# One FFN's units issued in written order on every engine, a queue order up to the first gates, and a norm without GpSimd

## The chip, the cores and the metric

The kernel runs as one program on one core of a Trainium2 chip. The core has a matrix engine (TensorE, PE in the rows; its weight loads are listed apart as PEld), three elementwise engines (VectorE = DVE, ScalarE = ACT, GpSimd = POOL), and a sync engine (SP) that here issues the DMAs. Each engine works through its own list of instructions in order; between the lists stand semaphores. The metric is the device time of one execution in microseconds (us), of which three runs of the kernel before gave 3029.19, 3029.55 and 3030.99: a median of 3029.55.

## The reference

One trunk layer of a diffusion backbone over 128 context and 1024 latent positions, 1152 rows of width 1024 in all. What matters here is the first half-step and what follows it:

```
h = modulate(rms_norm(x, norm_ffn1), sh1, sc1)              # sh, sc, g: SiLU(c) @ mod_w + mod_b
x = x + 0.5 * g1 * swiglu(h, ffn1_w_in, ffn1_w_out)          # swiglu: (silu(h @ Wg) * (h @ Wu)) @ w_out
h = modulate(rms_norm(x, norm_mix), sh2, sc2)
proj = h @ w_in                                              # u, v, q, kv, rotary key, two gates of 1024
...
```

The feed-forward width is 2816, so Wg and Wu are 1024 x 2816 each. Everything is fp32; the matrix engine works on a high and a low part of each operand, and a product is the sum of three passes (hi*hi, hi*lo, lo*hi). Each weight is therefore cast once (the high part, ACT, L150) and subtracted once (the low part, L151, POOL by default).

## The kernel before

**Tiling.** The rows lie in three blocks of 384 columns (b = 1, 2, 0 in FFN 1's order), and as two halves of 576. The feed-forward width is cut into 22 tiles of 128, called f. The up projection of a tile f is computed by a Strassen-Winograd scheme: seven products p = 1, 2, 6, 5, 7, 3, 4 of 4 x 128 rows of weights against 576 columns. A product is called a unit here: 24 matmuls of 128x288. For it the kernel forms four sums of the tile's weights on DVE (`make`, L547 to L550), casts the stationary part on ACT (L150) and takes its rest on POOL (L151).

**Stages.** `F1.up` first runs p1 and p2 of the first 9 tiles while the modulation and the first norm are still under way. Then a second loop runs the remaining units: 5 for each of the first 9 tiles, 7 for each of the other 13. Each step of it makes the operands of the unit five ahead, multiplies, drains (`done`) and calls `side1`. Behind it come the down projections (`F1.down`, four groups of tiles: 0 to 6, 7 to 10, 11 to 17, 18 to 21), which multiply the products a (kept in DRAM as `a_d`, loaded again into h10, h11, h20, ... by `a_load` and split by `a_split`) with w_out (`need_w`), and add the result to x (`x_load`). The drain of a down projection is L728. The last group is interleaved with the norm of the mixers (`done1`, `squares`, `norm_h`). Then come the first gate units, three for each block.

**PSUM.** The products of a tile share three pairs of banks in turn. p6 is copied out by ACT (L592) before p7 can use its pair; p7's drain on DVE (L599) must be over before p4 can start; p3 runs between the two on another pair. p1, p5 and p6 are drained by ACT (L592), p2, p7, p3 and p4 by DVE (L595, L599, L603, L613).

**Side work.** From tile 9 on `side1` also steps a generator `mods` that computes the other modulation vectors: 112 loads of 128x512 (`mraw`), for each two multiply-adds (macs) on DVE (L376 for the first, L378 for the others), then a fold over the partitions by two DMAs and two additions on POOL (L914), four transposes on PE (L204) and a sum on DVE (L371). Three steps are taken for each two units. On the last tile, f = 21, `F1.change(p)` runs behind each unit: it loads the first seven a tiles into the buffers of operands that are no longer needed, splits them, loads x, and prepares the first down weights.

**What sets the order.** PE runs in the written order throughout. For the other engines a tile scheduler sorts the instructions by its own estimates of when each is ready; `tc.manual_schedule(engines=...)` takes the named engines out of that, and they then issue in the order in which the program emits. In the kernel before, no other engine is taken out in this stretch.

Of the kernel before, what the change touches and what calls it, by code (L numbers as in the profile page):

```python
# [34 lines left out]
ADD_STEPS = 3  # L35
FOLD_STEPS = {1: 7, 2: 8}
FOLD_AT = 3
POOL_LO = {0: (0, 1, 3, 5), 1: (1, 3, 5, 7), 2: (1, 3, 5, 7)}
QK_SCALE = 192 ** -0.5

HT = T // 2
# [32 lines left out]
def tile_trunk(  # L74
# [314 lines left out]
    class Ffn:  # L389
# [5 lines left out]
        def __init__(self, which, order, wi, wo, early, chunks, wseq):  # L395
            self.which, self.order, self.wi, self.wo, self.early, self.chunks, self.wseq = which, order, wi, wo, early, chunks, wseq
            self.pools, self.hc, self.xq, self.acts, self.xt, self.wts = {}, {}, {}, {}, [], {}
            self.yt = self.ys = None
            self.yring, self.ycount = [], 0
            self.a_d = [dp.tile([P, T], F32, tag=f"a_d{which}_{f}", name=f"a_d{f}") for f in range(FT)]  # L400
            self.ya_d = [dp.tile([P, 2, HT], F32, tag=f"ya_d{which}_{f}", name=f"ya_d{f}") for f in range(early)]

            self.seq = [(f, p) for f0 in range(0, early, 3) for p in (1, 2) for f in range(f0, f0 + 3)]
            self.n_early = len(self.seq)
            self.seq += [(f, p) for f in range(FT) for p in (ORDER if f >= early else ORDER[2:])]
            self.first, self.raws, self.made, self.kept = {}, {}, {}, {}

        def slots(self, pl, *tags):
            for t in tags:
# [159 lines left out]
        def up(self, side):  # L569

            add, mult, early, seq, hc, ys, stores = ALU.add, ALU.mult, self.early, self.seq, self.hc, {}, []
            banks = [ps_two() for _ in range(3)]

            def kept_part(f):

                if f < early:
                    for i in (1, 2):
                        ys[f, i] = self.y_tile()
                        dma(ys[f, i], self.ya_d[f][:, i - 1])

            def silu(y):
                S.activation(out=y, in_=y, func=AF.Silu)

            def done(f, p, ps):
                while stores:
                    dma(*stores.pop())
                if p in (1, 5, 6):
                    y = ys[f, p] = self.y_tile()
                    if f < early:
                        V.tensor_tensor(out=two(y), in0=ps, in1=two(ys[f, 1]), op=add)  # L590
                    else:
                        S.copy(out=two(y), in_=ps)  # L592
                elif p == 2:
                    y = ys[f, 1]
                    V.tensor_tensor(out=two(y), in0=ps, in1=two(y), op=add)  # L595
                    silu(y)
                elif p == 7:
                    y = ys[f, 5]
                    V.tensor_tensor(out=two(y), in0=ps, in1=two(y), op=add)  # L599
                    kept_part(f + 1)  # L600
                elif p == 3:
                    u, y = ys.pop((f, 5)), ys.pop((f, 6))
                    V.tensor_tensor(out=two(y), in0=ps, in1=two(y), op=add)  # L603
                    silu(y)
                    G.tensor_tensor(out=y, in0=y, in1=u, op=mult)
                    stores.append((self.a_d[f][:, HT:T], y))
                else:
                    y = ys.pop((f, 1))
                    if f < early:
                        V.tensor_tensor(out=two(y), in0=ps, in1=two(y), op=add)  # L610
                        G.tensor_tensor(out=y, in0=y, in1=ys.pop((f, 2)), op=mult)
                    else:
                        V.tensor_tensor(out=two(y), in0=ps, in1=two(y), op=mult)  # L613
                    stores.append((self.a_d[f][:, 0:HT], y))
                    if f == FT - 1:
                        dma(*stores.pop())

            for i in range(6):
                self.make(i, V)
            for i0 in range(0, self.n_early, 6):  # L620
                for s in range(2):
                    for i in range(i0, i0 + 6):
                        f, p = seq[i]
                        self.ready(p, s)
                        ps = banks[f % 3]
                        self.product(ps, self.made[i], hc[p], p == 1, (s,))
                        if i % 2 == 0:
                            pair = self.yt.tile([P, 2, MV], F32, tag="ye", name="ye", bufs=3)
                        y = pair[:, i % 2]
                        S.activation(out=y, in_=ps[:, s, :MV], func=AF.Copy if p == 1 else AF.Silu)  # L630
                        dma(self.ya_d[f][:, p - 1, s * MV:s * MV + MV], y)
                        if s == 1:
                            self.make(i + 6)
            for i in range(self.n_early, len(seq)):
                f, p = seq[i]
                self.make(i + 5)
                self.ready(p, 0)
                if i == self.n_early:
                    kept_part(0)
                ba, bb, bc = (banks[(f + n) % 3] for n in range(3))  # L640
                ps = {1: ba, 2: bb, 6: ba, 5: bc, 7: ba, 3: bc, 4: ba}[p]
                self.product(ps, self.made[i], hc[p], p in (1, 2, 5) or (p == 6 and f < early))
                done(f, p, ps[:, :, :MV])
                side(f, p)
# [38 lines left out]
        def change(self, p):  # L683
# [4 lines left out]
            elif p == 2:  # L688
                self.a_load(2, "h20")
                self.a_load(3, "h21")  # L690
                self.a_split(0)
                self.a_split(1)
            elif p == 6:
                self.a_load(4, "h60")
                self.a_load(5, "h61")
                self.a_split(2)
            elif p == 5:
                self.a_load(6, "h50")
                self.a_split(3)
                self.need_w(0, 0)  # L700
            elif p == 7:
                self.x_load(0, "h70")
                self.x_load(1, "h71")
                self.a_split(4)
            elif p == 3:
                self.x_load(2, "h30")
                self.x_load(3, "h31")
                self.a_split(5)
                self.need_w(1, 0)
            else:  # L710
# [237 lines left out]
            F1.change(p)  # L948

    x_block(2)  # L950
    s_ps.close()
    s_ps = ps_pool("ps_w", wide=True)
    clk.later(X_FIRST[0], lambda: x_block(0, gap=gap1))
# [1 line left out]
    clk.flush()  # L955
    s_ps.close()
    s_ps = ps_pool("ps_d", 0, 8)
    into = {1: ("h51", "q0", "q1", "q2"), 2: ("h10", "h11", "h20", "h21", "h60", "h61", "h50"), 3: ("h51", "q0", "q1", "q2")}
    for c in range(3):
        f0, n = F1.chunks[c + 1]  # L960
# [32 lines left out]

    def done1(b, dt):
        if squares(b, dt):
            norm_rest(b, xT[b], r1s[b], 1, mixT, 1.5, 0.48, wait=7)

    win = w_in[0]
    chunk = {}
# [50 lines left out]
    for b in range(NB):  # L1050
        for i in range(3):
# [2 lines left out]
            gate_unit(i, b, loaded[i])  # L1054
            if i == 0:
                F1.x_store(b)
    s_fx.close()
    s_x = ctx.enter_context(ExitStack())
    xp_ = [pool(s_x, "xblocks", side="right")]
# [742 lines left out]
```

## Time and profile before

| | us |
|---|---|
| three runs, median | 3029.55 |
| profiled execution | 3026.47 |
| its span on the chip | 3024.7 |
| units of tiles 9 to 20 (p1 of f = 9 to p1 of f = 21) | 326.74 |
| f = 21 up to the first down projection | 29.36 |
| rest of the down projections up to the mixers' norm | 244.60 |
| the norm's end and the first gates | 73.90 |

The profiled execution is one of its own; its span is what the hardware profiler saw on the core, and 1.8 us lie around it. All positions (as 619.04) are us from the start of the span. A row of a window gives its length, the busy time of each engine with the number of instructions, the granted clock of PE as a share of the full 2.4 GHz, the busy share of the DMA engines and the GB/s moved. A row of the timeline gives the start, the length, the engine, the line and the operation; the bracket is the idle time ahead of it and what released it. A name that ends in a number is one tile.

### The profile page before, as it was taken

What the parts mean: (1) busy time and instruction counts of PE and PEld (TensorE: products, weight loads), DVE (VectorE), ACT (ScalarE), POOL (GpSimd) and SP (SyncE); (2) the same over time, 40 slices, a digit from 0 to 9 for tenths busy, and PEclk for the clock granted to TensorE, in tenths of its full rate; (3) what the DMA queues carried; (4) which work ended last, traced back from release to release, by engine and by line L of the source; (5) the groups of instructions that cost most, each with busy time, mean ns of one, the idle gap of its engine ahead of it and who ended that gap; (6) DMA issues with size and microseconds to landing.
All of it is one profiled execution on the core that took longest, in us unless ns stands there. A gap on an engine that the chain in (4) does not pass through costs nothing.

```text
span 3024.7 us, 47889 instructions
## 1 busy us (share of the span) xinstructions
PE 2880.4 (95%) x19102; PEld 2836.5 (94%) x19102; DVE 1416.5 (47%) x2774; ACT 988.8 (33%) x2073; POOL 990.4 (33%) x663
## 2 busy tenths in 40 slices
PE   7899888999997999999899999999989999999997
PEld 4799888899997999999899999999989999999997
DVE  4644766668526120027537667644364322242313
ACT  5622222232114231104226555521362333341113
POOL 4355445543323011110322212223135544442122
PEclk9999899999998999999999999999989999999999
DMA  8444444475322222211551111255234222244322
GB/s 289 144 128 130 130 125 128 126 246 176 103 72 81 57 64 89 76 35 39 174 152 40 57 32 48 76 181 155 87 124 131 81 66 93 68 157 134 100 71 98
DMA packets 355044, 330.16 MB, mean 109 GB/s; under 512 B 21172, under 2 KB 313380, under 8 KB 354436
## 3 DMA queue, kind: packets, MB, share of 16 engines
q1 hardware_dynamic: 354148, 325.13, 34.5%
q8 instruction: 150, 2.46, 0.3%
q0 software_dynamic: 672, 1.97, 0.2%
q14 instruction: 74, 0.61, 0.1%
HBM read 239.24 MB, written 81.76 MB: 106 GB/s over the span
## 4 chain that ended last, share of the span: by engine, by line
PE 76%; DVE 6%; issue 3%; DMA 2%; ACT 1%; POOL 1%; SPq 0%; DVEq 0%; POOLq 0%; ACTq 0%
PE ps_two L169 25%; PE ps_dn L169 18%; PE ps_up L169 18%; PE ps_w L169 6%; PE ps_s L169 3%; PE ps_s L1380 2%; PE ps_w L204 2%; DVE q L378 2%; DMA mraw<-q 1%; POOL wi L151 1%; PE ps_dn L1127 1%; PE ps_dn L204 1%; DMA mraw<-in_mod_w_dram 0%; DVE t L272 0%; PE ps_b L169 0%
## 5 line engine op out<-in xcount | busy, mean ns | idle before, releaser
L151 POOL TENSOR_TENSOR wi<-raw,wi 128x512 fp32r<-128x512 f32 (+2 forms) x382 | 639.8, 1679 | 1343.7 <-ACT wi L150 1259.7
L169 PE MATMUL ps_two<-h,wi 128*128 128x288 f32 x6336 | 877.2, 299 | 42.5 <-ACT q L592 14.6
L169 PEld LDWEIGHTS ps_two<-h,wi 128*128 128x128 f32 x6336 | 859.4, 191 | 52.8 <-ACT q L592 16.4
L150 ACT CAST wi<-raw 128x512 fp32r<-128x512 f32 (+2 forms) x401 | 290.2, 728 | 1048.9 <-PE ps_two L169 316.6
L169 PE MATMUL ps_dn<-h,wi 128*128 128x384 f32 x2304 | 418.8, 337 | 1.7 <-DVE q L613 1.7
L169 PEld LDWEIGHTS ps_dn<-h,wi 128*128 128x128 f32 x2304 | 402.5, 189 | 2.2 <-DVE q L613 2.2
L169 PE MATMUL ps_up<-h_hi,wi 128*128 128x384 f32 x1152 | 303.4, 340 | 0.0
L728 DVE SCALAR_TENSOR_TENSOR h<-ps_dn,modG,h 128x128 f32<-128x128 f32 (+2 forms) x224 | 108.7, 512 | 278.1 <-PE ps_dn L169 278.0
L169 PEld LDWEIGHTS ps_up<-h_hi,wi 128*128 128x128 f32 x1152 | 211.0, 189 | 0.0
L169 PE MATMUL ps_up<-h_lo,wi 128*128 128x384 f32 x576 | 195.1, 339 | 0.0
L378 DVE SCALAR_TENSOR_TENSOR q<-mraw,s,q 128x512 f32<-128x512 f32 x196 | 189.9, 1020 | 0.1
L169 PE MATMUL ps_two<-q,wi 128*128 128x288 f32 x1056 | 158.4, 309 | 30.0 <-DVE q L599 30.0
L169 PEld LDWEIGHTS ps_two<-q,wi 128*128 128x128 f32 x1056 | 152.8, 202 | 31.5 <-DVE q L599 31.5
L1451 POOL TENSOR_SCALAR p<-p,ast 128x1152 f32<-128x1152 f32 x64 | 79.2, 1237 | 303.6 <-PE ps_w L204 100.1
L169 PE MATMUL ps_up<-wi,h_hi 128*128 128x256 f32 (+1 forms) x864 | 160.8, 286 | 0.0
L169 PE MATMUL ps_dn<-q,wi 128*128 128x384 f32 x720 | 138.1, 338 | 0.0
L169 PE MATMUL ps_s<-kn,qn 128*128 128x384 f32 x576 | 136.9, 346 | 0.0
L150 ACT CAST pt<-ps_w 128x384 fp32r<-128x384 f32 x192 | 86.9, 488 | 145.5 <-PE ps_w L204 145.5
L169 PEld LDWEIGHTS ps_up<-wi,h_hi 128*128 128x128 f32 x864 | 133.6, 188 | 0.0
L169 PEld LDWEIGHTS ps_dn<-q,wi 128*128 128x128 f32 x720 | 126.5, 189 | 0.0
L169 PE MATMUL ps_up<-wi,h_lo 128*128 128x256 f32 (+1 forms) x432 | 122.7, 284 | 0.0
L169 PE MATMUL ps_w<-pt,v 128*128 128x256 f32 x864 | 118.4, 288 | 0.0
(263 smaller groups left out, 4180.3 us busy)
## 6 DMA issues: line engine op xcount, KB each, us to landing
raw<-in_ffn_w_in_dram SPq DMA_DIRECT2D x103, 512.0 KB, 3.9
mraw<-in_mod_w_dram SPq DMA_DIRECT2D x112, 256.0 KB, 2.8
a_d<-q SPq DMA_DIRECT2D x88, 288.0 KB, 2.5
h<-a_d SPq DMA_DIRECT2D x32, 576.0 KB, 8.0
raw<-in_w_in_dram SPq DMA_DIRECT2D x34, 512.0 KB, 3.9
raw<-in_ffn_w_out_dram SPq DMA_DIRECT2D x32, 448.0 KB, 3.8
h<-x_d SPq DMA_DIRECT2D x24, 384.0 KB, 7.6
g_d<-t SPq DMA_DIRECT2D x48, 192.0 KB, 2.1
```

The source lines that it names most:

```text
L150: S.copy(out=hi, in_=src)
L151: (lo_eng or G).tensor_tensor(out=lo, in0=src, in1=f32(hi), op=ALU.subtract)
L169: nc.tensor.matmul(ps, lhsT=l[i], rhs=r[j], start=start and i == j, stop=stop and i == 1, skip_group_check=more)
L204: nc.tensor.transpose(out, in_, ident)
L378: V.scalar_tensor_tensor(out=ac, in0=w, scalar=s2[:, j, cd:cd + 1], in1=ac, op0=ALU.mult, op1=ALU.add)
L728: V.scalar_tensor_tensor(out=xs, in0=ps[:, c0:c1], scalar=modG[:, self.which, cd, dt:dt + 1], in1=xs, op0=ALU.mult, op1=ALU.add)
L1127: nc.tensor.matmul(pm[:, i, :], lhsT=vb[b][:, i, g * P:g * P + P], rhs=wsT[:, g, :], start=True, stop=True)
L1380: nc.tensor.matmul(ps, lhsT=q2[h][:, ts_], rhs=kab[j][:, c0:c1], start=False, stop=j == 1)
L1451: G.tensor_scalar(out=p, in0=p, scalar1=rc, scalar2=0.0, op0=ALU.mult, op1=ALU.add)
```

## The change

The second loop of `up` becomes a function `units`. For FFN 1 it runs under `tc.manual_schedule` for DVE, ACT, POOL and SP, so that they issue in the written order; FFN 2 keeps the scheduler. SP stays in written order from the end of `F1.up` to the end of the first gate units. On the last tile the splits of the a tiles come one or two units later, and the first down weight is asked for after p7 instead of p5. The norm of the mixers computes the low parts of all eight k tiles on DVE (L290), where four of the eight were POOL's (L287) with one more step on ACT. In `done1` the norm's steps of blocks 1 and 2 come later. Code that the diff leaves alone moves five lines down behind the new function, eight behind the new queue order.

```diff
--- before.py
+++ after.py
@@ -35,7 +35,7 @@
 ADD_STEPS = 3
 FOLD_STEPS = {1: 7, 2: 8}
 FOLD_AT = 3
-POOL_LO = {0: (0, 1, 3, 5), 1: (1, 3, 5, 7), 2: (1, 3, 5, 7)}
+POOL_LO = {0: (0, 1, 3, 5), 1: (), 2: (1, 3, 5, 7)}
 QK_SCALE = 192 ** -0.5
 
 HT = T // 2
@@ -404,6 +404,7 @@
             self.n_early = len(self.seq)
             self.seq += [(f, p) for f in range(FT) for p in (ORDER if f >= early else ORDER[2:])]
             self.first, self.raws, self.made, self.kept = {}, {}, {}, {}
+            self.ordered = None
 
         def slots(self, pl, *tags):
             for t in tags:
@@ -631,12 +632,16 @@
                         dma(self.ya_d[f][:, p - 1, s * MV:s * MV + MV], y)
                         if s == 1:
                             self.make(i + 6)
+            self.ready(6, 0)
+            kept_part(0)
+            with tc.manual_schedule(engines=self.ordered) if self.ordered else ExitStack():
+                self.units(seq, banks, done, side)
+
+        def units(self, seq, banks, done, side):
+            hc, early = self.hc, self.early
             for i in range(self.n_early, len(seq)):
                 f, p = seq[i]
                 self.make(i + 5)
-                self.ready(p, 0)
-                if i == self.n_early:
-                    kept_part(0)
                 ba, bb, bc = (banks[(f + n) % 3] for n in range(3))
                 ps = {1: ba, 2: bb, 6: ba, 5: bc, 7: ba, 3: bc, 4: ba}[p]
                 self.product(ps, self.made[i], hc[p], p in (1, 2, 5) or (p == 6 and f < early))
@@ -688,23 +693,23 @@
             elif p == 2:
                 self.a_load(2, "h20")
                 self.a_load(3, "h21")
-                self.a_split(0)
-                self.a_split(1)
             elif p == 6:
                 self.a_load(4, "h60")
                 self.a_load(5, "h61")
-                self.a_split(2)
+                self.a_split(0)
             elif p == 5:
                 self.a_load(6, "h50")
-                self.a_split(3)
-                self.need_w(0, 0)
+                self.a_split(1)
+                self.a_split(2)
             elif p == 7:
                 self.x_load(0, "h70")
                 self.x_load(1, "h71")
-                self.a_split(4)
+                self.need_w(0, 0)
+                self.a_split(3)
             elif p == 3:
                 self.x_load(2, "h30")
                 self.x_load(3, "h31")
+                self.a_split(4)
                 self.a_split(5)
                 self.need_w(1, 0)
             else:
@@ -948,6 +953,7 @@
             F1.change(p)
 
     x_block(2)
+    F1.ordered = {mybir.EngineType.DVE, mybir.EngineType.Activation, mybir.EngineType.Pool, mybir.EngineType.SP}
     s_ps.close()
     s_ps = ps_pool("ps_w", wide=True)
     clk.later(X_FIRST[0], lambda: x_block(0, gap=gap1))
@@ -955,6 +961,8 @@
     clk.flush()
     s_ps.close()
     s_ps = ps_pool("ps_d", 0, 8)
+    s_o = ExitStack()
+    s_o.enter_context(tc.manual_schedule(engines={mybir.EngineType.SP}))
     into = {1: ("h51", "q0", "q1", "q2"), 2: ("h10", "h11", "h20", "h21", "h60", "h61", "h50"), 3: ("h51", "q0", "q1", "q2")}
     for c in range(3):
         f0, n = F1.chunks[c + 1]
@@ -993,7 +1001,7 @@
 
     def done1(b, dt):
         if squares(b, dt):
-            norm_rest(b, xT[b], r1s[b], 1, mixT, 1.5, 0.48, wait=7)
+            norm_rest(b, xT[b], r1s[b], 1, mixT, (1.5, 6.0, 8.0)[b], 0.48, wait=7)
 
     win = w_in[0]
     chunk = {}
@@ -1054,6 +1062,7 @@
             gate_unit(i, b, loaded[i])
             if i == 0:
                 F1.x_store(b)
+    s_o.close()
     s_fx.close()
     s_x = ctx.enter_context(ExitStack())
     xp_ = [pool(s_x, "xblocks", side="right")]
```

Three places of the order. The first is DVE in the units of one tile f, from the start of the sums or the drain of p2 (L595 before, L596 after) on; L547 to L550 (L548 to L551 after) are the sums of the next tile, L599 (L600) is p7's drain, which p4 waits for. Before:

```order
L547 TENSOR_TENSOR s_3228<-raw 128x512
L378 SCALAR_TENSOR_TENSOR q_1202<-mraw,s_114,q_1202 128x512
L595 TENSOR_TENSOR q_1201<-ps_two,q_1201 128x576
L548 TENSOR_TENSOR raw<-raw 128x512
L378 SCALAR_TENSOR_TENSOR q_1202<-mraw,s_114,q_1202 128x512
L549 TENSOR_TENSOR raw<-s_3228,raw 128x512
L378 SCALAR_TENSOR_TENSOR q_1202<-mraw,s_114,q_1202 128x512 x4
L550 TENSOR_TENSOR raw<-raw 128x512
L378 SCALAR_TENSOR_TENSOR q_1202<-mraw,s_114,q_1202 128x512 x5
L599 TENSOR_TENSOR q_1201<-ps_two,q_1201 128x576
L603 TENSOR_TENSOR q_1201<-ps_two,q_1201 128x576
L613 TENSOR_TENSOR q_1201<-ps_two,q_1201 128x576
```

After:

```order
L596 TENSOR_TENSOR q_1201<-ps_two,q_1201 128x576
L378 SCALAR_TENSOR_TENSOR q_1202<-mraw,s_114,q_1202 128x512 x4
L548 TENSOR_TENSOR s_3230<-raw 128x512
L549 TENSOR_TENSOR raw<-raw 128x512
L550 TENSOR_TENSOR raw<-s_3230,raw 128x512
L551 TENSOR_TENSOR raw<-raw 128x512
L600 TENSOR_TENSOR q_1201<-ps_two,q_1201 128x576
L378 SCALAR_TENSOR_TENSOR q_1202<-mraw,s_114,q_1202 128x512
L376 TENSOR_SCALAR q_1202<-mraw,s_114 128x512
L604 TENSOR_TENSOR q_1201<-ps_two,q_1201 128x576
L376 TENSOR_SCALAR q_1202<-mraw,s_114 128x512
L614 TENSOR_TENSOR q_1201<-ps_two,q_1201 128x576
```

Between the drain of p2 and that of p7 stood ten macs and three of the sums; now there are four macs and the four sums, or in about every second tile five macs, the four sums and a short group from L371 on. The other macs stand behind the drains of p7, p3 and p4.

The second is SP at the end of the units. `raw<-in_ffn_w_out` is a weight of the down projection, h10 and on are buffers that receive the a tiles, h70 and h71 receive x. Before:

```order
L88 DMA a_d19_134<-q2_1201 128x576
L88 DMA raw_5827<-in_ffn1_w_out_dram 128x7x128
L88 DMA mraw_2907<-q3_1202 64x512 x2
L88 DMA mraw_2903<-in_mod_w_dram 128x512
L88 DMA a_d20_135<-q2_1201 128x576
L88 DMA mraw_2904<-in_mod_w_dram 128x512
L88 DMA a_d20_135<-q2_1201 128x576
L88 DMA raw_5911<-in_ffn1_w_out_dram 128x7x128
L88 DMA h10_5716<-a_d0_115 128x1152
L88 DMA h11_5718<-a_d1_116 128x1152
```

After:

```order
L88 DMA mraw_2909<-q3_1202 64x512 x2
L88 DMA mraw_2908<-in_mod_w_dram 128x512
L88 DMA h50_5821<-a_d6_121 128x1152
L88 DMA h70_5853<-x_d0_71 128x2x384
L88 DMA h70_5853<-x_d1_72 128x2x384
L88 DMA h70_5853<-x_d2_73 128x2x384
L88 DMA h71_5857<-x_d0_71 128x2x384
L88 DMA h71_5857<-x_d1_72 128x2x384
L88 DMA h71_5857<-x_d2_73 128x2x384
L88 DMA raw_5861<-in_ffn1_w_out_dram 128x7x128
L88 DMA mraw_2905<-in_mod_w_dram 128x512
```

The first weight of the down projection stood ahead of all loads of a tiles; now it stands behind seven of them and the six loads of x into h70 and h71, which have to wait until PE is done with p7.

The third is DVE in the norm of the mixers, ahead of the sum L230 of block 1's squares, for which PE's transposes wait; L290 (h_lo0) are the low parts of block 0, L728 (L733) are drains of the last down projections. Before:

```order
L272 SCALAR_TENSOR_TENSOR t384_8258<-h31_5905,modA_112,t384_8176 128x128
L272 SCALAR_TENSOR_TENSOR t384_8258<-h31_5905,modA_112,t384_8176 128x256
L290 SCALAR_TENSOR_TENSOR h_lo0_8182<-t384_8247,modT_111,h_hi0_8181 128x128
L290 SCALAR_TENSOR_TENSOR h_lo0_8182<-t384_8247,modT_111,h_hi0_8181 128x256
L728 SCALAR_TENSOR_TENSOR h31_5905<-ps_dn_8243,modG_113,h31_5905 128x384
L728 SCALAR_TENSOR_TENSOR h71_5863<-ps_dn_8280,modG_113,h71_5863 128x384
L226 TENSOR_TENSOR r1_8140<-r1_8140,t384_8277 128x384
L230 TENSOR_TENSOR r1_8138<-r1_8138,r1_8140 128x384
```

After:

```order
L290 SCALAR_TENSOR_TENSOR h_lo0_8187<-t384_8252,modT_111,h_hi0_8186 128x128
L290 SCALAR_TENSOR_TENSOR h_lo0_8187<-t384_8252,modT_111,h_hi0_8186 128x256
L290 SCALAR_TENSOR_TENSOR h_lo0_8187<-t384_8262,modT_111,h_hi0_8186 128x128
L290 SCALAR_TENSOR_TENSOR h_lo0_8187<-t384_8262,modT_111,h_hi0_8186 128x256
L733 SCALAR_TENSOR_TENSOR h31_5905<-ps_dn_8248,modG_113,h31_5905 128x384
L733 SCALAR_TENSOR_TENSOR h71_5857<-ps_dn_8285,modG_113,h71_5857 128x384
L733 SCALAR_TENSOR_TENSOR h30_5901<-ps_dn_8315,modG_113,h30_5901 128x384
L226 TENSOR_TENSOR r1_8145<-r1_8145,t384_8282 128x384
L733 SCALAR_TENSOR_TENSOR h30_5901<-ps_dn_8332,modG_113,h30_5901 128x384
L230 TENSOR_TENSOR r1_8143<-r1_8143,r1_8145 128x384
```

Ahead of L230 stood eight low parts of block 0, and now there are sixteen, and two drains more.

## Rows read from the trace of the kernel before

**Rows 1.** Windows: stretch, length, busy time by engine, PE clock, DMA share, GB/s.

```profile
292.30:619.04 326.74, 287.85 (x2047) 285.33 (x2046) 227.28 (x272) 85.62 (x143) 163.78 (x113) 0.93 0.42 125
619.04:648.40 29.36, 24.23 (x171) 23.77 (x169) 26.24 (x24) 14.91 (x18) 12.05 (x7) 0.94 0.80 276
648.40:893.00 244.60, 244.60 (x1420) 244.35 (x1421) 139.72 (x220) 40.31 (x47) 75.87 (x44) 1.00 0.47 145
893.00:966.90 73.90, 55.42 (x305) 54.29 (x304) 53.29 (x112) 35.34 (x71) 28.05 (x22) 0.88 0.27 86
885.00:907.00 22.00, 22.00 (x129) 22.00 (x128) 8.79 (x20) 5.18 (x9) 4.34 (x4) 1.00 0.44 138
```

**Rows 2.** Timeline, DVE, units at the full clock: drains of p7 of two tiles.

```profile
205.38 0.76 DVE L599 TENSOR_TENSOR q<-ps_two,q 128x576 f32<-128x576 f32 x1 [2.42 <-PE ps_two L169]
...
221.48 0.76 DVE L599 TENSOR_TENSOR q<-ps_two,q 128x576 f32<-128x576 f32 x1 [2.42 <-PE ps_two L169]
```

**Rows 3.** Waits, 292.3 to 647.5: total us, times, longest.

```profile
PE ps_two L169 <- DVE q L599: 28.5, 5, 6.2
...
DVE s L547 <- DMA raw<-in_ffn_w_in_dram: 28.1, 7, 6.0
...
PE ps_two L169 <- ACT q L592: 14.6, 5, 4.3
```

**Rows 4.** Timeline, 310 to 328: DVE and PE around one drain of p7.

```profile
312.40 0.74 DVE L378 SCALAR_TENSOR_TENSOR q<-mraw,s,q 128x512 f32<-128x512 f32 x1
...
313.86 6.86 DVE L378 SCALAR_TENSOR_TENSOR q<-mraw,s,q 128x512 f32<-128x512 f32 x4
...
321.44 5.55 PE L169 MATMUL ps_two<-q,wi 128*128 128x288 f32 x24 [6.04 <-DVE q L599]
```

**Rows 5.** Lines by form, 292.3 to 647.5: busy us, mean ns, idle before, releaser.

```profile
L378 DVE SCALAR_TENSOR_TENSOR q<-mraw,s,q 128x512 f32<-128x512 f32 x136 | 137.9, 1067 | 0.1
...
L548 DVE TENSOR_TENSOR raw<-raw 128x512 f32<-128x512 f32 x12 | 10.1, 839 | 0.6
...
L371 DVE TENSOR_REDUCE msum<-ps_dn 128x8 f32<-128x512 f32 x7 | 4.8, 686 | 6.1 <-PE ps_dn L204 6.1
...
L151 DVE TENSOR_TENSOR h<-h 128x1152 fp32r<-128x1152 f32 x7 | 10.5, 1536 | 2.7 <-ACT h L150 2.6
...
L150 ACT CAST h<-h 128x1152 fp32r<-128x1152 f32 x7 | 7.7, 1149 | 0.0
...
L204 PE MATMUL ps_dn<-ident,mraw 128*128 128x128 f32 x28 | 4.2, 272 | 0.0
```

**Rows 6.** Timeline, 616 to 650: the last tile and the first down projection.

```profile
619.04 12.85 PE L169 MATMUL ps_two<-h,wi 128*128 128x288 f32 x96
...
625.63 0.95 ACT L150 CAST wi<-raw 128x896 fp32r<-128x896 f32 x1 [2.06 <-issue]
...
641.19 8.50 SPq L88 DMA_DIRECT2D h<-x_d  x12
...
648.35 1.83 PE L169 MATMUL ps_dn<-h,wi 128*128 128x384 f32 x9 [0.85 <-DVE q L613]
```

**Rows 7.** DMA issues, 600 to 680: KB each, median us to landing.

```profile
raw<-in_ffn_w_out_dram SPq DMA_DIRECT2D x8, 448.0 KB, 6.2
```

**Rows 8.** Timeline, 918 to 958: the mixers' norm and PE's waits.

```profile
921.74 2.53 POOL L151 TENSOR_TENSOR wi<-raw,wi 128x1024 fp32r<-128x1024 f32 x1
...
922.51 3.04 DVE L290 SCALAR_TENSOR_TENSOR h_lo<-t,modT,h_hi 128x128 fp32r<-128x128 f32 x2
...
927.53 0.73 DVE L290 SCALAR_TENSOR_TENSOR h_lo<-t,modT,h_hi 128x128 fp32r<-128x128 f32 x2
...
930.93 0.90 PE L204 MATMUL ps_dn<-ident,r 128*128 128x128 f32 x3 [9.28 <-DVE r L230]
...
946.66 0.38 PE L242 MATMUL ps_dn<-ones,r 128*128 128x1 f32 x2 [4.19 <-POOL r L226]
...
951.68 2.29 PE L242 MATMUL ps_dn<-ones,r 128*128 128x1 f32 x10 [4.63 <-DVE r L226]
```

## The prediction

> **What bounds the kernel now.** I read the windows first, stage by stage. In the down projections PE is busy for 244.60 of 244.60 us at the full clock: nothing can be won there [rows 1]. In the two stages ahead of it and in the one behind it PE has gaps, and those are the stages that the change touches.
>
> The units of tiles 9 to 20 take 326.74 us, with PE busy for 287.85 and a granted clock of 0.93 [rows 1]. What they need is seen where no engine was late: two drains of p7 lie 221.48 - 205.38 = 16.10 us apart with five units between them, so a unit is 3.22 us at the full clock [rows 2]. From p1 of f = 9 to p1 of f = 21 there are 12 x 7 = 84 units, 270.5 us, and 28 transposes of 4.2 us in all [rows 5], of which I count 3.6: 274.1. So 52.6 us are lost: 38.9 idle, and 13.7 in matmuls at the lower clock, which is granted after idle time.
>
> The waits say who is late: p4 waits for p7's drain (28.5 us, longest 6.2), and p7 for the copy of p6 (14.6) [rows 3]. The timeline shows why. DVE does macs from 313.86 for 6.86 us without a gap, then the drain, and PE starts p4 6.04 us late and then takes 5.55 us for 24 matmuls instead of 3.22 [rows 4]. DVE isn't short of time: it is busy for 227.28 of 326.74 us [rows 1]. It has the wrong work in front.
>
> The last tile takes 29.36 us up to the first down projection [rows 1], for 7 x 3.22 = 22.5 us of work: 6.9 lost. In the norm and the first gates, PE is busy for 55.42 of 73.90 us [rows 1]: 18.5 idle. Its 305 instructions there take 0.182 us on average; just before they take 22.00 / 129 = 0.171 [rows 1]; the difference, 3.4 us, is the lower clock. Lost: 21.9. Nearly all the idle time is three waits: 9.28 us for L230 of block 1, 4.19 and 4.63 for L226 of block 2 [rows 8].
>
> **The change part by part.**
>
> *The units in written order.* Between p2's drain and p7's there were ten macs and three sums, 10 x 1.07 + 3 x 0.84 = 13.2 us [rows 5], with idle time for data on top; now four macs and four sums, 7.6 us, or with a fifth mac and a group from L371 (0.69 [rows 5], and four short operations that I put at 1.6) 11.0. PE needs 3 x 3.22 = 9.66 us from p2's end to p7's, and p3 covers one more unit before p4 needs the drain: 12.9 us, less the drains of p2 and p7, each 0.76 [rows 2], leaves 11.4. The light tiles have 3.8 us to spare and the heavy ones 0.4, so I expect some waits of about 1 us in the heavy ones: 4 us in the stretch with what they cost in clock. In total DVE would be busy for 227.28 and POOL for 163.78 us of about 278 [rows 1], 82% and 59%. Gain: 52.6 - 4 = 48.6. The bounds: everything lost comes back (52.6), or nothing does (0); 48.6 is near the first because the work between two drains now fits, by rows.
>
> Here a rule speaks against the change. The pair L290 takes 0.73 us where POOL is quiet and 3.04 where POOL does a 2.53 us subtraction beside it [rows 8]; likewise a mac takes 0.74 us in one place and 1.07 on average [rows 4, 5]. The Trainium skill ("SBUF — State Buffer", section "SBUF: two separate sides") has it that GpSimd and a VectorE operation with two SBUF inputs exclude each other on a shared port pair for the whole instruction. If POOL's same work lies in 278 us instead of 327, the waiting part of the macs, 136 x 0.33 = 45 us [rows 4, 5], would grow by 327/278 to 53: some 8 us more on DVE, of which only the heavy tiles' share, about 4, would reach PE. By this estimate the gain would be 45.
>
> *The end of the units.* Before, the first down weight was cast at 625.63, 6.6 us after p1 of f = 21 began [rows 6]. Now its load stands on SP behind the six loads of x into h70 and h71, which wait for p7: 5 x 3.22 = 16.1 us after p1. Twelve such issues took 8.50 us [rows 6], so six take 4.3: the weight is issued at 20.4 and lands after 6.2 [rows 7] at 26.6. Then everything is in order. On ACT: its cast 0.95 [rows 6], then that of h21, 1.15 [rows 5]: 28.7. On DVE: the split of h21, 1.54 [rows 5], and p3's drain: 31.0. ACT's silu (put at a drain's length) and the casts of h60 and h61 end at 34.0, DVE's three macs in between at 34.2, its two splits at 37.3, and only then p4's drain, 38.0, on whose bank the first down projection waits. If the load takes as long as it did where the queue was emptier, everything is some 2 us earlier; I take 37. PE has nothing to do from 22.5 on, so it idles 14.5 us, and after such a gap the clock is low for a while: the 9.28 us gap cost 1.9 of the 3.4 us above, so 2. New: 39, against 29.4: a loss of 10. The bounds: a gain of 6 (no wait at all) and a loss of 12.
>
> *The queue order on SP in the down projections* moves loads only where PE waits for none [rows 1]; the cover is one weight's load of 6.2 us [rows 7] beside 30 us for eight steps of it. Nothing; if the cover is gone, one load.
>
> *The norm.* PE ran dry at 930.93 - 9.28 = 921.65 [rows 8]. Block 1's step comes 4.5 later on the kernel's own clock of PE work (6.0 instead of 1.5), so PE arrives at 926.2. DVE has four pairs of L290 more ahead of L230, 2.9 us at 0.73, and is spared part of the 2.3 us that POOL cost a pair [rows 8]: L230 ends between 931 and 934. The wait is 5 to 8, say 6. Block 2's step comes 6.5 later, and both its waits, 8.8 us [rows 8], are over by then. Left: 6, about 2 for transposes and products that wait for each other, 2 for the clock: 10 of 21.9, a gain of 12 (6 to 19).
>
> The sum: 48.6 - 10 + 12 = 50.6. The profiled execution took 3026.5; 2975.9 on its base. The median of three runs is 3.1 above it: 2979.
>
> **The rivals.**
>
> *A, DVE stays behind.* The written order puts each weight's sums and splits where they must wait for loads and POOL in turn, and an in-order engine can't use such a wait. If each of 12 tiles still loses 3 us, 36 us of the gain are gone: 3015. For it: DVE waits for weights 28.1 us in the units already [rows 3], and the heavy tiles have 0.4 us to spare. Against it: the light ones have 3.8.
>
> *B, the boundary costs nothing*, because x or the weight lands sooner or the next bank is free: 10 back, and 3 to 5 from the old gap: 2965. For it: the load itself is short. Against it: p4's drain stands behind the splits whatever the load does.
>
> *C, slower.* One mechanism: the four sums stand ahead of p7's drain, and the first of them reads a weight whose load stands on SP behind the store of an a tile, which waits for POOL's product. A late weight then holds p7's drain, and so PE, in each tile. A wait for a weight was up to 6.0 us [rows 3]. At 6.0 for each of 12 tiles, PE would lose 72 us and, as in the stall above, about 2.3 in clock each time, 28: 100 instead of 52.6, so with the other two terms 3029.6 + 47 + 10 - 12 = 3075. It decides from 4.4 us a tile on, clock included, thus from a wait of about 2.1: there (4.4 x 12 = 52.6) the units gain nothing, and the other two terms nearly cancel. For it: the queue is now strictly in order. Against it: the load of the weight is asked for a whole tile ahead.
>
> *D, no change.* If the scheduler's order was near the written one where it matters, and the stalls come from the amount of work, the units stay at 326.7 and the time at 3029.6 + 10 - 12 = 3028. Against it: ten macs between two drains became four or five.
>
> **How the numbers follow.** The forecast (2979) has 0.55, A 0.18, B 0.14, C 0.08, D 0.05. The forecast's own range goes from 2968 (gates at their best) to 2992. The range of 8 in 10 takes in B and A and leaves out C, D and the edges: 2958 to 3018. Runs of this kernel differ by 1.8 us, and 0.2% or 6 us is about what can be told from no change. Faster by more: the forecast, B and nearly all of A, 0.87. Same: D and a part of C, 0.05. Slower: 0.08.
>
> **What would show it.** The units from p1 of f = 9 to p1 of f = 21: 278 us with a clock above 0.98, and waits of PE for p7's drain under 10 us. If that window is above 300, A; above 327, C. A gap of PE of 12 to 16 us ahead of the first down projection, ended by p4's drain; none, B. The window from the norm's begin to the end of the first gates of the last block 12 us shorter, with one wait for L230 of 5 to 8 us. What would make it wrong: waits of PE for weights' casts or splits, which before had none of length, or a second stage that is slower although nothing in it was moved.

## The result

The changed kernel takes 2983.09 us (median of four runs, 2980.64 to 2986.1) against 3029.37 of before (3025.32 to 3030.99): a ratio of 0.985, 95% interval 0.9833 to 0.9867. It is faster by 46 us; 50 were forecast (2979), and the time lies inside the range.

The two traces divide the kernel at the same instructions: p1 of f = 9, p1 of f = 21, the first down projection, the first sum of squares of the mixers' norm (L242) and the first matmul of 128x256 behind the gates. Windows of the changed kernel (length, busy time of PE, PEld, DVE, ACT, POOL, clock, DMA share, GB/s), first the units, then the last tile, the down projections, and the norm with the gates:

```profile
290.89:567.06 276.17, 272.76 (x2047) 272.29 (x2045) 212.71 (x250) 84.77 (x142) 160.30 (x111) 0.99 0.44 138
567.06:610.41 43.35, 22.37 (x171) 22.17 (x169) 26.60 (x25) 15.71 (x19) 16.22 (x9) 0.80 0.88 294
610.41:862.00 251.59, 251.59 (x1451) 251.34 (x1452) 161.91 (x246) 41.67 (x49) 78.62 (x44) 0.99 0.45 135
870.78:944.06 73.28, 64.08 (x364) 62.92 (x364) 52.33 (x118) 33.54 (x65) 15.20 (x9) 0.95 0.32 108
```

The last of these as it was before:

```profile
907.16:991.61 84.45, 65.97 (x365) 64.84 (x365) 51.17 (x102) 38.39 (x77) 27.74 (x21) 0.90 0.26 84
```

| stretch | before | after | gain | forecast |
|---|---|---|---|---|
| up to p1 of f = 9 | 292.29 | 290.89 | 1.4 | 0 |
| units of tiles 9 to 20 [rows 1, first] | 326.75 | 276.17 | 50.6 | 48.6 |
| last tile [rows 1, second] | 29.31 | 43.35 | -14.0 | -10 |
| down projections up to L242 | 258.81 | 260.37 | -1.6 | in the -10 |
| norm and gates | 84.45 | 73.28 | 11.2 | 12 |
| the rest of the span | 2033.1 | 2034.8 | -1.8 | 0 |
| sum | | | 45.8 | 50.6 |

In the units PE is idle for 276.17 - 272.76 = 3.4 us, where it was 38.9, and the granted clock is 0.99 instead of 0.93. All that PE waits for between the units and the gates in the changed kernel (total us, times, longest):

```profile
PE ps_dn L169 <- DVE q L614: 21.0, 1, 21.0
PE ps_dn L169 <- DVE h L733: 6.6, 1, 6.6
PE ps_two L169 <- ACT q L593: 3.3, 1, 3.3
PE ps_dn L204 <- DVE st L213: 2.2, 1, 2.2
PE ps_dn L242 <- DVE r L226: 0.4, 1, 0.4
```

No wait for p7's drain is left ([rows 3] had 28.5 us). Of the waits for a copy, 14.6 us in [rows 3], one of 3.3 is left. They were named after ACT, but in four of the five (12.5 us) it was p6's copy, and that stood on ACT behind the silu (L582) of p2's result, which waited for p2's drain on DVE, and that stood behind macs. The longest of the four, before the change:

```profile
625.15 6.95 DVE L378 SCALAR_TENSOR_TENSOR q<-mraw,s,q 128x512 f32<-128x512 f32 x7
...
632.02 0.74 DVE L595 TENSOR_TENSOR q<-ps_two,q 128x576 f32<-128x576 f32 x1
...
632.80 0.68 ACT L582 ACTIVATE q<-q 128x576 f32<-128x576 f32 x1 [6.22 <-DVE q L595]
633.39 2.19 ACT L150 CAST h<-h 128x1152 fp32r<-128x1152 f32 x2
...
635.48 0.63 ACT L592 COPY q<-ps_two 128x576 f32<-128x576 f32 x1
...
636.16 8.17 PE L169 MATMUL ps_two<-h,wi 128*128 128x288 f32 x48 [4.28 <-ACT q L592]
```

The macs did get longer, as the argument on the shared port had it: by form, between 290.89 and 605 us,

```profile
L378 DVE SCALAR_TENSOR_TENSOR q<-mraw,s,q 128x512 f32<-128x512 f32 x117 | 134.1, 1186 | 6.6 <-DMA mraw<-in_mod_w_dram 6.6
L548 DVE TENSOR_TENSOR s<-raw 128x512 f32<-128x512 f32 x12 | 12.6, 1049 | 0.0
L376 DVE TENSOR_SCALAR q<-mraw,s 128x512 f32<-128x512 f32 x18 | 11.2, 644 | 0.0
```

so 145.3 us for 135 macs (L378 and L376), 1.08 each, where the 136 and 20 of before took 137.9 ([rows 5]) and 21.2, 1.02 each. The rise is that of L378, which reads two tensors: 1186 ns instead of 1067. L376, which reads one, fell from 1072 to 644. No L378 of this stretch without a POOL instruction beside it took more than 0.75 us. That agrees with the Trainium skill ("SBUF — State Buffer", section "SBUF: two separate sides"): with POOL's work in less time, more macs meet it. It cost DVE some 14 us in L378 (117 x 0.119), where 8 were estimated, and some 8 over all macs (135 x 0.06). PE's waits show none of it, where 4 were put down to it.

The one loss is the last tile. The timeline, from the loads of x on to the first down projection:

```profile
583.12 4.19 SPq L88 DMA_DIRECT2D h<-x_d  x6
587.35 0.47 SPq L88 DMA_DIRECT2D raw<-in_ffn_w_out_dram  x1
...
596.76 0.94 ACT L150 CAST wi<-raw 128x896 fp32r<-128x896 f32 x1 [14.02 <-DMA raw<-in_ffn_w_out_dram]
597.60 1.15 ACT L150 CAST h<-h 128x1152 fp32r<-128x1152 f32 x1
...
598.78 2.34 DVE L151 TENSOR_TENSOR h<-h 128x1152 fp32r<-128x1152 f32 x1 [13.11 <-ACT h L150]
601.04 0.74 DVE L604 TENSOR_TENSOR q<-ps_two,q 128x576 f32<-128x576 f32 x1
601.71 3.21 DVE L378 SCALAR_TENSOR_TENSOR q<-mraw,s,q 128x512 f32<-128x512 f32 x3
...
604.85 4.75 DVE L151 TENSOR_TENSOR h<-h 128x1152 fp32r<-128x1152 f32 x2
...
609.52 0.74 DVE L614 TENSOR_TENSOR q<-ps_two,q 128x576 f32<-128x576 f32 x1
...
610.41 5.82 PE L169 MATMUL ps_dn<-h,wi 128*128 128x384 f32 x23 [20.98 <-DVE q L614]
```

The first down weight is issued behind six loads of x, 20.3 us after p1 of f = 21, and lands 9.4 us later. ACT has waited 14.02 us for it, with the cast of h21 behind it; DVE has waited 13.11 us for that cast, with p3's drain, three macs, two splits and p4's drain behind it; and PE has waited 20.98 us for p4's drain. It is the chain that was forecast, link by link, but it ends 43.35 us after p1 instead of 38.0 (37 was taken): 3.2 for the load (9.4 instead of 6.2), and about 2 for splits that take 2.3 us each instead of 1.54.

In the norm, the wait that remained is not the one that was named:

```profile
890.26 4.14 DVE L290 SCALAR_TENSOR_TENSOR h_lo<-t,modT,h_hi 128x128 fp32r<-128x128 f32 x6
894.32 1.65 DVE L733 SCALAR_TENSOR_TENSOR h<-ps_dn,modG,h 128x384 f32<-128x384 f32 x3
894.98 1.33 PE L169 MATMUL ps_dn<-h,wi 128*128 128x384 f32 x3 [6.59 <-DVE h L733]
...
905.57 0.54 PE L204 MATMUL ps_dn<-ident,st 128*128 128x128 f32 x3 [2.24 <-DVE st L213]
```

Six low parts (L290) stand in a row in front of three drains (L733), and PE waits 6.59 us for the first of these, since the bank that it is to write next must be drained by it. L230 follows while PE works. The waits for block 2 ([rows 8]: 4.19 and 4.63) are gone.

### The profile page after: what moved, and what is told of

It is laid out like the page before. It is cut to its first block, busy times and chain, and to the rows that moved or that the text cites. A ratio compares the mean times of both kernels' runs of the same rounds, so it can differ in the third digit from the quotient of the medians.

```text
span 2978.9 us, 47869 instructions
## 1 busy us (share of the span) xinstructions
PE 2862.8 (96%) x19102; PEld 2821.9 (95%) x19102; DVE 1429.3 (48%) x2790; ACT 982.6 (33%) x2061; POOL 980.5 (33%) x651
## 4 chain that ended last, share of the span: by engine, by line
PE 81%; DVE 3%; issue 2%; DMA 1%; POOL 1%; ACT 1%; SPq 0%; DVEq 0%; POOLq 0%; ACTq 0%
PE ps_two L169 29%; PE ps_dn L169 18%; PE ps_up L169 18%; PE ps_w L169 6%; PE ps_s L169 3%; PE ps_s L1389 2%; PE ps_w L204 2%; POOL wi L151 1%; DMA h<-a_d 1%; PE ps_dn L1136 1%; PE ps_dn L204 0%; PE ps_b L169 0%; ACT q L461 0%; DVE h_lo L290 0%; DMA raw<-in_ffn_w_in_dram 0%
## 5 line engine op out<-in xcount | busy, mean ns | idle before, releaser
L169 PEld LDWEIGHTS ps_dn<-h,wi 128*128 128x128 f32 x2304 | 403.7, 189 | 29.2 <-ACT wi L150 21.2
L733 DVE SCALAR_TENSOR_TENSOR h<-ps_dn,modG,h 128x128 f32<-128x128 f32 (+2 forms) x224 | 108.8, 512 | 268.9 <-PE ps_dn L169 268.8
L378 DVE SCALAR_TENSOR_TENSOR q<-mraw,s,q 128x512 f32<-128x512 f32 x196 | 206.1, 1094 | 9.6 <-DMA mraw<-in_mod_w_dram 9.5
L169 PE MATMUL ps_two<-q,wi 128*128 128x288 f32 x1056 | 146.9, 294 | 1.6 <-DVE q L600 1.6
L169 PEld LDWEIGHTS ps_two<-q,wi 128*128 128x128 f32 x1056 | 142.1, 188 | 1.8 <-DVE q L600 1.8
```

Source lines behind the costliest of these rows:

```text
L169: nc.tensor.matmul(ps, lhsT=l[i], rhs=r[j], start=start and i == j, stop=stop and i == 1, skip_group_check=more)
L378: V.scalar_tensor_tensor(out=ac, in0=w, scalar=s2[:, j, cd:cd + 1], in1=ac, op0=ALU.mult, op1=ALU.add)
L733: V.scalar_tensor_tensor(out=xs, in0=ps[:, c0:c1], scalar=modG[:, self.which, cd, dt:dt + 1], in1=xs, op0=ALU.mult, op1=ALU.add)
```

## The experiments

All were timed beside the kernel before on the same chip. Twelve kernels, each from the changed kernel unless said otherwise.

### Which part brings what

**The units alone.** The norm, its steps and SP's order behind the units as before.

```diff
-POOL_LO = {0: (0, 1, 3, 5), 1: (), 2: (1, 3, 5, 7)}
+POOL_LO = {0: (0, 1, 3, 5), 1: (1, 3, 5, 7), 2: (1, 3, 5, 7)}
...
-    s_o = ExitStack()
-    s_o.enter_context(tc.manual_schedule(engines={mybir.EngineType.SP}))
...
-            norm_rest(b, xT[b], r1s[b], 1, mixT, (1.5, 6.0, 8.0)[b], 0.48, wait=7)
+            norm_rest(b, xT[b], r1s[b], 1, mixT, 1.5, 0.48, wait=7)
...
-    s_o.close()
```

> The changed kernel with the mixers' norm, its steps and the queue order after the units as before; only the units (with their new placing on the last tile) are in written order. Theory: the two parts add up. The units give back 50 us, the end of the last tile costs 14 to 16, and the gates stay at their old 22 us of loss: time 2993 to 2996. Rival: the gates gain from the earlier arrival of something in the units or in the queue order too; then the time is under 2990.

2992.76 us, ratio 0.9877 (0.9859 to 0.9895). The units take 276.1 us, the last tile 44.4, norm and gates 84.5, as before. The time is just under the theory's 2993 to 2996, and the parts are as it had them.

**The gates alone.** `change` and the scheduling of the units as before.

```diff
-    F1.ordered = {mybir.EngineType.DVE, mybir.EngineType.Activation, mybir.EngineType.Pool, mybir.EngineType.SP}
...
```

> The reverse: units and last tile as before (scheduled), and only the mixers' norm on DVE, its later steps and the queue order after the units. Theory: 11 us better than before, all of it between the first sum of squares and the third gate unit: 3018 to 3020, with the units at 326 us. Rival: the gates' part of the gain hangs on the units' order; then within 4 us of before.

3014.34 us, ratio 0.9951 (0.9936 to 0.9967). Norm and gates take 73.5 us, the 11 expected; another 4 come from the last tile (25.2 us instead of 29.3), where the scheduler placed things otherwise, which was not expected and puts the time 4 us under the theory's 3018 to 3020. The units take 325.0 us, and the stalls of before are there:

```profile
PE ps_two L169 <- DVE q L600: 29.3, 6, 6.4
PE ps_two L169 <- ACT q L593: 11.3, 5, 3.0
```

**The steps and the low parts, one by one.** First the low parts on POOL again, then the steps at 1.5 again.

```diff
-POOL_LO = {0: (0, 1, 3, 5), 1: (), 2: (1, 3, 5, 7)}
+POOL_LO = {0: (0, 1, 3, 5), 1: (1, 3, 5, 7), 2: (1, 3, 5, 7)}
```

> The changed kernel with the mixers' norm as before (four of eight low parts on POOL), the later steps kept. Theory: most of the gates' 11 us comes from the later steps (block 2's two waits are gone by them alone), and the low parts on DVE bring at most 3 us, since the sixteen of block 0 now hold the drain L733 that PE waits 6.6 us for: time 2980 to 2986. Rival: POOL's subtraction beside DVE's two-operand operations is what made the norm late; then 2988 or more.

```diff
-            norm_rest(b, xT[b], r1s[b], 1, mixT, (1.5, 6.0, 8.0)[b], 0.48, wait=7)
+            norm_rest(b, xT[b], r1s[b], 1, mixT, 1.5, 0.48, wait=7)
```

> The changed kernel with the norm's steps at 1.5 for all blocks again, the low parts on DVE kept. Theory: block 2's two waits (4.2 and 4.6 us before) and block 1's 9 us come back for the most part, since PE reaches them early again: 2990 to 2994. Rival: the low parts on DVE alone make the sums ready in time; then 2983 to 2986.

With the low parts on POOL: 2988.07 us (2980.37 to 2989.48), and 73.2 us for norm and gates, the same as the changed kernel's 73.3. The wait for the drain is shorter, but a wait for L230 is added:

```profile
PE ps_dn L169 <- DVE h L733: 4.1, 1, 4.1
PE ps_dn L204 <- DVE r L230: 2.6, 1, 2.6
```

In the trace the stretch that this edit touches is as long as without it. But the traced execution is the fastest of the four (2980.37); the others took 2987.19 to 2989.48, so the median lies 5 us above the changed kernel's, and where those 5 us are no trace shows. With the steps at 1.5: 2996.33 us (2991.33 to 3001.14), 2 us over the theory's range, and 84.2 us for norm and gates, with waits like those of before back:

```profile
PE ps_dn L204 <- DVE r L230: 9.3, 1, 9.3
PE ps_dn L242 <- DVE r L226: 5.6, 2, 5.3
PE ps_dn L242 <- POOL r L226: 3.0, 1, 3.0
```

So, by the traces, the later steps are the whole gain of this part (84.2 to 73.3), and neither the low parts on DVE nor SP's order, which the last kernel keeps, adds to it. Whether the low parts are worth anything to the whole time stays open: the traced execution falls where the theory had it (2980 to 2986), and the median where the rival had it (2988 or more).

### Whose order matters in the units

```diff
-    F1.ordered = {mybir.EngineType.DVE, mybir.EngineType.Activation, mybir.EngineType.Pool, mybir.EngineType.SP}
+    F1.ordered = {mybir.EngineType.DVE}
```

> The changed kernel with only DVE in written order in the units; ACT, POOL and SP are scheduled. Theory: DVE's order (four or five macs instead of ten between the drains of p2 and p7) is what took the stalls away, so the units stay near 276 to 285 us, and only the last tile changes with the order of the loads: 2970 to 2992. Rival: the loads' or the casts' order is as necessary; then PE waits again for drains or weights and the units take over 300 us, time above 3005.

In the other, `{DVE, Activation, Pool}`:

> The changed kernel with DVE, ACT and POOL in written order in the units and SP scheduled. Theory: the same units (276 to 280 us), since PE never waited for a load there; the last tile's gap stays if the scheduler too puts the first down weight behind the loads of x, and shrinks if not: 2968 to 2985. Rival: the scheduler sends the loads of the macs in bunches of eight, so that DVE, now bound to the written order, waits for weights or macs and p7's drain is late: units over 290 us.

DVE alone: 2964.99 us, ratio 0.9785 (0.977 to 0.9801). Without SP: 2966.46 us, 0.9791 (0.9773 to 0.9808). Both are faster than the changed kernel. PE's busy time between 290 and 560 us in both, DVE alone first:

```profile
290.00:560.00 270.00, 268.57 (x2034) 268.10 (x2034) 214.62 (x243) 88.08 (x143) 165.89 (x111) 1.00 0.47 139
```

```profile
290.00:560.00 270.00, 269.93 (x2047) 269.70 (x2046) 213.72 (x251) 85.69 (x144) 159.99 (x111) 1.00 0.47 140
```

From p1 of f = 9 to p1 of f = 21 they take 271.6 and 269.9 us. Both came out better than expected, in time (2970 to 2992 and 2968 to 2985) and in the units (276 us at least). DVE's order is enough to take the stalls away: the wait for p7's drain is gone in both, and 1.3 and 0 us are left of the waits for a copy. Whether the order of the other three without DVE's would do the same was not run, nor were the macs moved by themselves. The written order of ACT and POOL costs nothing in the units, and that of SP costs 6 us: in the changed kernel the store of an a tile stands on SP behind a weight's load, goes out at 295.29 us, and ACT's copy of p1 in the first tile has to wait for its landing. So PE waits 3.34 us before p6, and then has a granted clock of 0.83 between 300 and 320 us. Of the 17 to 18 us over the changed kernel, most lie in the last tile: 28.5 and 30.4 us instead of 43.4, since SP, scheduled, loads the first down weight early again.

### What holds PE in the last tile

Two theories: the weight's load holds ACT's queue and all behind it, or the splits of h60 and h61 in front of p4's drain hold DVE. The weight at p5 as before, then in front of all loads at p1, then only the splits moved, then the weight at p1 and the splits moved:

```diff
             elif p == 5:
                 self.a_load(6, "h50")
+                self.need_w(0, 0)
...
             elif p == 7:
...
-                self.need_w(0, 0)
```

> The changed kernel with only the first down weight asked for after p5 again (it was after p7). Theory: the 21 us gap ahead of the first down projection comes from that weight's load, which stood behind six loads of x and held ACT's queue, and with it DVE's. Now it is issued at about 13 us after p1 of the last tile, lands some 6 to 9 later, and holds the casts of h11 and h20 in the meantime, so p4 starts up to 6 us late, but the rest follows at once: first down projection at 33 to 36 us instead of 43.3, time 2974 to 2977. Rival: the splits of h60 and h61 ahead of p4's drain hold PE whatever the weight does; then the gap shrinks by less than 4 us and the time stays at 2980 to 2983.

```diff
             if p == 1:
+                self.need_w(0, 0)
                 self.a_load(0, "h10")
...
             elif p == 7:
...
-                self.need_w(0, 0)
```

> The changed kernel with only the first down weight moved to the front of what p1 of the last tile issues (ahead of all loads of a tiles). Theory: with the weight there early nothing holds ACT; p4's drain still stands behind three macs and the splits of h60 and h61 on DVE, so PE waits some 5 us instead of 21: first down projection at about 27 us after p1, time about 2966. Rival (the splits in front of the drain are the cause, not the weight): the wait stays above 15 us and the time at 2980 or more.

```diff
             elif p == 3:
...
-                self.a_split(4)
-                self.a_split(5)
                 self.need_w(1, 0)
             else:
+                self.a_split(4)
+                self.a_split(5)
                 self.a_split(6)
```

> The changed kernel with only the splits of h60 and h61 moved behind p4's drain; the weight stays behind the loads of x. Theory (the weight): p3's drain still stands behind the split of h21, whose cast waits on ACT behind the weight's; p4's drain comes some 5 us earlier than in the changed kernel, but PE then waits for the splits instead: 2979 to 2983. Rival (the splits): the gap falls to under 6 us, time about 2968.

The fourth kernel has the second and the third of these edits.

> Both edits: the weight in front at p1, the splits of h60 and h61 behind p4's drain. Theory: the first down projection starts within 3 us of p4's end (25 us after p1), but the splits of h60 and h61 now stand behind a sum (L371) that waits for PE's transposes, so PE waits 2 to 5 us for h60 within the first down projection. Time 2962 to 2967, the same as with the weight alone or up to 4 us better.

Times and lengths in us; the last tile is counted from p1 of f = 21 to the first down projection.

| | time | last tile | PE's waits there |
|---|---|---|---|
| changed kernel | 2983.09 | 43.4 | 21.0 |
| weight at p5 | 2980.0 | 41.5 | 11.2 + 5.1 |
| weight at p1 | 2968.44 | 30.0 | 7.6 |
| splits moved | 2977.98 | 39.4 | 17.0 |
| both | 2973.99 | 25.4 | 3.0, and 6.3 + 1.7 later |

The weight at p1 decides it: 13 of the 21 us go, as the theory of the weight said (2966 expected, 2968 measured; the first down projection at 30.0 us, where about 27 were expected). The splits alone are worth 4 us of the wait, where it had 5; the wait for the splits that it expected in their place did not come, and the time is 1 us under its range. The weight at p5 came 3 us above its range, at a time that the rival had named. The trace shows another cause than the rival's: p4 was to start up to 6 us late and it was 11, since the load took 9.3 us there and ACT held the casts of h11 and h20 behind it. PE's two waits in that kernel:

```profile
PE ps_two L169 <- DVE q L600: 11.2, 1, 11.2
PE ps_dn L169 <- DVE q L614: 5.1, 1, 5.1
```

The same mechanism spoils the kernel with both edits. Its first down projection starts early, after a wait of 2.95 us, but the casts of h60 and h61 now stand on ACT behind that of the *second* down weight, which is late in the same way:

```profile
604.97 0.94 ACT L150 CAST wi<-raw 128x896 fp32r<-128x896 f32 x1 [15.71 <-DMA raw<-in_ffn_w_out_dram]
605.81 3.25 ACT L150 CAST h<-h 128x1152 fp32r<-128x1152 f32 x3
...
607.01 0.69 PE L169 MATMUL ps_dn<-h,wi 128*128 128x384 f32 x1 [6.35 <-ACT h L150]
```

It was expected at 2962 to 2967 and came in at 2973.99; the wait for h60 was expected behind a sum on DVE (L371), and it came from ACT. In these kernels ACT was held by whichever weight's cast had a late load.

### Further than the changed kernel

With DVE alone in order, p4's drain stands behind macs and splits. Without macs behind p7 and p3 of the last tile:

```diff
-        if f >= F1.early:
+        if f >= F1.early and not (f == FT - 1 and p in (7, 3)):
             some(*MOD_UP)
```

> DVE alone in written order in the units, and no macs of the modulation behind p7 and p3 of the last tile (they run in the down projections instead). Theory: p4's drain stood behind three macs and two splits on DVE, 3.2 and 3.1 us, and PE waited 5.9 us for it; without the macs it waits 2 to 3 and nothing else is late: 2961 to 2963, against 2965 with DVE alone in written order. Rival: the drain waits for the loads and casts of h60 and h61, not for DVE's time; then 2964 to 2966.

2963.29 us (2959.95 to 2966.28), ratio 0.9783 (0.9768 to 0.9797). The last tile takes 27.6 us; the wait for p4's drain is 4.0 us, where 2 to 3 were expected, and waits of 0.7 us are added. It has the lowest median of all, but is not clear of the kernel with DVE alone (2964.99; ratios 0.9783 and 0.9785), so time doesn't tell the theory (2961 to 2963) from its rival (2964 to 2966). The trace has the drain behind p3's drain and two splits on DVE, 4.25 us, without a wait for a load, as the theory had it.

Then the steps of block 0's norm spread out, to bring the drains forward:

```diff
-            norm_rest(b, xT[b], r1s[b], 1, mixT, (1.5, 6.0, 8.0)[b], 0.48, wait=7)
+            norm_rest(b, xT[b], r1s[b], 1, mixT, (1.5, 6.0, 8.0)[b], (0.7, 0.48, 0.48)[b], wait=7)
```

> The kernel of the last run (DVE alone in written order in the units, no macs behind p7 and p3 of the last tile) with the steps of block 0's norm spread at 0.7 instead of 0.48, so that the down projections' drains stand between the low parts on DVE instead of behind them. Theory: the 6.6 us wait for the drain L733 comes from the low parts in front of it; it falls under 3 us and the first gates start 3 to 4 us earlier: 2958 to 2961. Rival: the low parts are then late for block 0's first gate unit, and the wait only moves there: 2962 to 2965.

2969.17 us, ratio 0.9802 (0.9788 to 0.9815): 6 us above the last kernel's median, of which the traces show 3.6 in norm and gates (78.7 us instead of 75.1). The wait for the drain is gone, and another takes its place:

```profile
PE ps_dn L204 <- DVE st L213: 13.5, 1, 13.5
```

Block 0's remaining low parts and the steps they are made from now stand between L230 and the short steps from L247 to L213, whose result PE transposes. The theory on the cause of the 6.6 us held, since the wait went with the low parts in front of the drain; the expectation of a gain (2958 to 2961) did not. The rival was right that the wait only moves, but had it at block 0's first gate unit and the time at 2962 to 2965.

## Why the prediction was right

- *Units: 48.6 forecast, 50.6 measured.* The mechanism held: with four or five macs between two drains, no drain is late, and DVE alone in order suffices. No heavy tile loses anything; what remains is at the first tile of the stretch, a wait of 3.3 us for a copy (L593) and slow matmuls behind it (96 in 15.59 us, where 96 take 12.86 in the next tiles). That the size is so near is in part luck. The 3.22 us for a unit were read in tiles of five units; in the last tile of the changed kernel six units take 586.10 - 567.06 = 19.04 us, 3.17 each, and the kernel without SP's order runs the whole stretch in 269.9 us, not 274.1. So 56.8 us could be won, more than the bound of 52.6, and the changed kernel still loses 6.2, where 4 were expected and in another place.
- *Last tile: -10 forecast, -15.6 measured* (14.0 there and 1.6 in the down projections behind it). Right in the chain, too small in size: the load's term was 6.2 us and measured 9.4, and a split's 1.54 and measured up to 2.4. The loss lies outside the stated bound of 12, and the gap of 21.0 us above the 12 to 16 that were to show it.
- *Queue order on SP: 0.* In the down projections PE is busy for 251.59 of 251.59 us. Right there; in the units, where no price was put on SP's order, it cost 6 us, as the kernel without it shows.
- *Norm and gates: 12 forecast, 11.2 measured.* The size is right, one step isn't: "DVE has four pairs of L290 more ahead of L230" had L230 end the wait; it was the drain ahead of it, on the same queue (6.59 us, and 2.24 for the short steps behind it). So the 6 us came out right for a wait that was not named. And the text left open how much is owed to the low parts on DVE; in the traces of this stretch it is nothing.
- *Rivals.* A (DVE stays behind) and C (a late weight holds p7's drain) have no trace: no wait of PE for p7's drain, and DVE's first sum (L548), which waited 28.1 us for weights [rows 3], waits for none. B (no gap at the boundary) is refuted by 21.0 us. D is refuted by the units alone.
- The terms' errors (+2.0, -5.6, -0.8, and +1.4 and -1.8 in stretches that the change doesn't touch) add up to -4.8 us; in part they offset each other. The last 1.8 were not followed up.

## What to carry to other kernels

When PE waits for a drain while the draining engine is far from full, look for what stands ahead of the drain in that engine's list, and order that one engine by hand; ordering the others as well can cost more than it brings. A wait that is named after another engine can lead back to the same list, as the copies on ACT did. On an engine in written order, a cast or split whose load is late holds all that stands behind it, so each load must be issued early enough, or its consumer written behind whatever others wait for. Where PE reaches a step before its operands are ready, place that step later behind other PE work: two numbers were worth 11 us here.

## What was not expected of the hardware

A 448 KB weight that landed 6.2 us after its issue before (a median of eight [rows 7]) took 9.4 us behind six loads of x, 9.3 with seven loads of a tiles in front of it and six of x behind, and at most 5.4 ahead of them all (the weight at p1); why was not looked into. A split of 128x1152 on DVE took 1.34 us alone (the weight at p5) and 2.34 beside POOL's 2.08 us subtraction (the changed kernel).
